# Another order of side work in an attention stage, a copy in two pieces and a power moved between two passes

## The chip, the cores and the metric

The kernel runs on one core of a Trainium2 chip. The metric is device time in microseconds (us) for one launch. A core has five engines with queues of their own: TensorE (PE) for matrix products, with its weight loads shown apart as PEld; VectorE (DVE); ScalarE (ACT); GpSimd (POOL); and SyncE (SP), which here only issues DMAs. Each engine works through its queue in order, and semaphores make it wait for the others.

## The reference

One inference step of a two-layer trunk for 128 context tokens and 512 latent tokens, width 1024, in float32. Layer 0 is gated grouped-query attention (16 heads, 4 key/value heads, head width 64), layer 1 a gated linear recurrence (HGRN2) in two directions. Cut to what matters here:

```python
for i in range(DEPTH):
    sh_p, sc_p, g_p = _adaln(c_ctx, ada_w[i], ada_b[i])        # shift, scale, gate
    hp = xp * (1.0 + sc_p) + sh_p                              # latent tokens alike
    if i % N_MIXERS == 0:
        out_p, kp, vp = _attn_context(hp, attn_w_in[j], ...)   # q, k normalised, rotary
        out_s = _attn_latent(hs, cache_k[:, j], cache_v[:, j], attn_w_in[j], ...)
    else:
        out_p, sp_fw, sp_bw = _rec_mix(hp, zeros, zeros, rec_w_in[j], ...)
        out_s, _, _ = _rec_mix(hs, state_rec[:, j, 0], state_rec[:, j, 1], ...)
    xp = _layer_norm(DEEPNORM_ALPHA * xp + g_p * out_p, ln_gain[i], ln_bias[i])
    xs = _layer_norm(DEEPNORM_ALPHA * xs + g_s * out_s, ln_gain[i], ln_bias[i])
```

Attention's inner step is `softmax(q @ k.T / sqrt(d)) @ v`; its result is multiplied by `silu(g)` and projected. The recurrence's result is RMS-normalised per head, multiplied by `silu(g)` and projected.

## The kernel before, in words

Tokens are tiled in five tiles of 128 (tile 4 holds the context tokens). Most products are made with both operands split into a high part of reduced precision and a low remainder, as three matmuls: high by high, high by low, low by high. So weights and activations are "split" before use: a copy to the high part on ACT (L242, L1133, L1562) and a subtraction for the low part on DVE or POOL (L243, L1134, L1563).

**Attention.** Work goes by units: one query head with 256 queries, or the context queries of four heads. A unit has two fronts and a back. A front makes a score tile `sc` on PE (L896, L897), its negative row maximum `nm` on DVE (L991), the exponentials `p` with their sums `su` on ACT (L996), the reciprocal `rc` on DVE (L1001) and the scaling of `p` on POOL (L1002). The back transposes `p` on PE into `pt` (L1009), copies it to `pts` on ACT or, for the last quarter, on DVE (L901), and for each pair of units multiplies with the values into `pot` (L923). The product with the gate, `gs` (L928), is put off by `D_OUTS` steps. `att_gen` runs fronts two units ahead of backs.

**Side work.** Between these steps `weave` takes steps from a list of other jobs: for each of three further groups of four heads the q projection (`q_gen`: `qmm` on PE, L363 to L365, then norm and rotary on DVE, a split `qs`, transposes `qps`, L707, and the copy to `X`); inside it, at the spots of `FILL_AT`, the modulation matmuls (`ada_gen`, `adaps`, L286) or, for the third group, ten column jobs (`cols_gen`, `spill`, L335, each a 128x1024 multiply with accumulation on DVE); then the first output weights (`wohi`, `wolo`) and the splits of `gs` into `hhi` and `hlo` (L1133, L1134). How many side steps follow each attention step is written as a string of digits, `SIDE_AT`. A compile-time scheduler then orders all of this first half on every engine, so the string shifts rows in all queues.

Score tiles share two PSUM buffers, `pt`, `qmm`, `qps` and `adaps` share three, `pot` has one.

**The tail.** The last head's recurrence ends with five transposes `oT` (L1561), the copy to `ghi` on ACT (L1562) and the remainder `glo` on DVE (L1563). The output projection `outp` (L1185 to L1187) has by then done all other heads for tiles 0 to 2. Class `Out` makes residual and layer norm: the product with the gate (L1231), the residual sum (L1234), sums on ACT (L1241, L1249), small statistics (L1245, L1246), a power on POOL for the reciprocal deviation (`rstdl`: L192 on DVE, then L193), and two passes over the two halves (L1268, L1270), with a DMA for each half (L1271).

Of the kernel before, what the change touches and what calls it, by code (L numbers as in the profile page):

```python
# [11 lines left out]
F32 = mybir.dt.float32  # L12
F32R = mybir.dt.float32r
U8 = mybir.dt.uint8
AF = mybir.ActivationFunctionType
ALU = mybir.AluOpType
AX = mybir.AxisListType

P = 128
# [4 lines left out]
NT = TT * P  # L24
# [4 lines left out]
RH = 8  # L29
# [4 lines left out]
ALPHA = 4.0 ** 0.25  # L34
HALVES = ((0, 320), (320, 640))
RAW_AHEAD = 2
FILL_AT = {1: '0a0b0e2e4e', 2: '0b0e2e4e', 3: '0b0e4e'}
LEAD = (1, 1)
RAW_START = 8
EARLY = 2  # L40
WARM = (8, 2, 3)
D_SCALE = 2
D_OUTS = 2
SIDE_T = 2.2
SIDE_AT = (
    "0101101011111000110110101101011011010110111001101021010010110110"
    "1001011010210101200101002011110100110101101002011000121110001101"
    "0110110101101002002110010110101101102002011101000001201101011")
D_GLA = 6.0
D_LEV = 2.3  # L50
D_KT = 2.0
# [78 lines left out]
def drain(gen):  # L130
    for _ in gen:
        pass
# [3 lines left out]
def hybrid_step(ctx: ExitStack, tc: tile.TileContext, a: dict, o: dict):  # L136
    nc = tc.nc
# [11 lines left out]
    def bank2(name):  # L149
        return pools["b2"].tile([P, 2, 512], F32, tag="b2", name=name)  # L150
# [38 lines left out]
    def rsqrt(out, in_, scale, eps, op=ALU.mult):  # L189
        n = in_.shape[-1]  # L190
        t = tiny.tile([P, NKV * TT], F32, tag="rs", name="rs_t")
        nc.vector.tensor_scalar(t[:, :n], in_, scale, eps, op, ALU.add)  # L192
        nc.gpsimd.tensor_tensor(out, t[:, :n], mhalf[:, :n], ALU.pow)  # L193
# [524 lines left out]
    def q_gen(c, X, fill):  # L718

        w = Weights("attn_w_in", c, (nc.vector, nc.vector), tuple(last_split))  # L720
        yield
        spots = {FILL_AT[c][i:i + 2] for i in range(0, len(FILL_AT[c]), 2)}
        pend = None
# [182 lines left out]
    def defer(n, fn):  # L906
        if n == 0:
            fn()
        else:
            later.append([n, fn])  # L910
# [14 lines left out]
    def av_out(pot, gt):  # L925
        tv = pot[:, :CW]
        tv = tv.rearrange("p (a b) -> p a b", a=2) if len(gt.shape) == 3 else tv
        defer(D_OUTS, lambda: tc.keep_in_program_order(nc.vector.tensor_tensor(gt, tv, gt, ALU.mult)))  # L928

# [206 lines left out]
    def split_gs(ks):  # L1136
        for k in ks:
            split_act(hhi[:, k, :], hlo[:, k, :], gs[:, k, :], nc.gpsimd if k < 6 else nc.vector)
            yield
# [49 lines left out]
    class Norm:  # L1189
# [15 lines left out]
        def finish(self):  # L1205
            y = self.y
            mv = tiny.tile([P, 2], F32, tag="mv", name="mv")
            nc.vector.bn_aggr(mv, self.st[:].rearrange("p a b -> p (a b)"))
            rt = tiny.tile([P, 8], F32, tag="rstd", name="rstdl")
            rstd = rt[:, 0:1]  # L1210
            rsqrt(rstd, mv[:, 1:2], 1.0, LN_EPS)
            for nh in range(2):
                s = slice(nh * 512, (nh + 1) * 512)
                nc.vector.tensor_scalar(y[:, s], y[:, s], mv[:, 0:1], rstd, ALU.subtract, ALU.mult)
            nc.sync.dma_start(x1d[self.tt], y)

    class Out:
# [43 lines left out]
                self.mean, self.op = self.st[:, 0, 1:2], ALU.add  # L1261
                rsqrt(self.rs, self.st[:, 1, 1:2], self.st[:, 1, 2:3], LN_EPS, ALU.add)

        def finish(self):
            x, y = self.x, self.y
            hs = [slice(nh * 512, (nh + 1) * 512) for nh in range(2)]
            for s in hs:
                nc.vector.scalar_tensor_tensor(x[:, s], y[:, s], self.mean, lng[:, s], self.op, ALU.mult)  # L1268
            for nh, s in enumerate(hs):
                nc.vector.scalar_tensor_tensor(x[:, s], x[:, s], self.rs, lnb[:, s], ALU.mult, ALU.add)  # L1270
                (nc.scalar if self.last and nh else nc.sync).dma_start(yd[self.tt][:, s], x[:, s])  # L1271

    drain(split_gs(range(6, 8)))
    drain(wo_gen(0, PIECES[4:], wob))
# [23 lines left out]
    def wide(ps):  # L1298
        return ps[:].rearrange("p a b -> p (a b)")
# [134 lines left out]
    ghi = hp.tile([P, KT, NT], F32R, tag="hhi", name="ghi")  # L1434
    glo = hp.tile([P, KT, NT], F32R, tag="hlo", name="glo")
# [4 lines left out]
    ngain = h1p.tile([P, 1], F32, name="ngain")  # L1440
# [5 lines left out]
    def gla_gen(h, H):  # L1446
# [25 lines left out]
        for lev in range(7):  # L1472
            nb = NT // (2 * w)
            pt = wide(bank2("lv"))
# [23 lines left out]
            if lev == 4:  # L1498
                pt = wide(bank2("dg"))
# [27 lines left out]
        for i in range(3):  # L1527
            nc.vector.scalar_tensor_tensor(S[:, 0, i + 1, :], S[:, 0, i, :], cur[:, i:i + 1], spv[:, i * P:(i + 1) * P],
                                           ALU.mult, ALU.add)
            c = 3 - i  # L1530
# [27 lines left out]
        pt = bank2("oT")  # L1558
        for c in range(TT):
            cc = slice(c * P, (c + 1) * P)  # L1560
            nc.tensor.transpose(wide(pt)[:, cc], on[:, cc], ident)  # L1561
        nc.scalar.activation(ghi[:, h, :], wide(pt)[:, :NT], AF.Copy, scale=ngain[:, 0:1])  # L1562
        nc.vector.scalar_tensor_tensor(glo[:, h, :], wide(pt)[:, :NT], ngain[:, 0:1], ghi[:, h, :].bitcast(F32),  # L1563
                                       ALU.mult, ALU.subtract)
        yield 0.0

    class Residual:
# [48 lines left out]
    for h in range(RH):  # L1616
        H = {} if h else H
        for dt in proj_gen(h, H, False) if h else first:
            lane.advance(dt)
        lane.add(gla_gen(h, H))  # L1620
# [70 lines left out]
    o3 = Out(3, outs[3])  # L1691
# [11 lines left out]
    o2 = Out(2, outs[2])  # L1703
# [2 lines left out]
    out_mms(o4.ps, 4, 0, ghi, glo)  # L1706
    for out in (o3, o2):
        out.spread()
    for out in (o3, o2):
        out.rstd()  # L1710
        out.finish()
    o4.half(both[0])
    for c in (slice(0, CW), slice(CW, 512)):
        if c.start:
# [88 lines left out]
```

## Time and profile before

| | us |
|---|---|
| median of the runs (3) | 839.59 |
| lowest and highest | 836.24, 839.99 |
| the profiled execution, own time | 837.36 |
| its span, first to last instruction | 835.6 |

The page gives, for each engine, its busy time and share of the span, and the busy share in 40 equal slices. A group's row gives line, engine, operation, names (out<-in), shapes and count, then busy time, mean ns of one, and the engine's idle time before it with the releaser. A row of the timeline gives start, duration and, in brackets, how long the engine stood idle just before and what ended that.

### The profile page before, as it was taken

To read this page: it belongs to the slowest core of one execution; us is meant where nothing else is said; L and a number is where in the kernel's file an instruction comes from. 1 tells how busy PE (TensorE), PEld (TensorE's weight loads), DVE (VectorE), ACT (ScalarE), POOL (GpSimd) and SP (SyncE) were. 2 spreads that over 40 slices of the span, in tenths; PEclk is the share of its full clock that TensorE was granted. 3 is DMA by queue.
4 is the path that set the end of the run, shared out by engine and by line. 5 is a ranking of instruction groups with operands and counts; after the bars stand their busy time and mean duration, and the time that the engine had idled before them with its cause. 6 is when DMAs were issued, how large, how long until landed. Compare 5 with 4: busy or idle time off the path is not lost.

```text
span 835.6 us, 19217 instructions
## 1 busy us (share of the span) xinstructions
PE 806.7 (97%) x8025; PEld 727.9 (87%) x8025; DVE 563.3 (67%) x996; ACT 386.6 (46%) x782; POOL 212.5 (25%) x261
## 2 busy tenths in 40 slices
PE   8999999999999889999999999999999999999994
PEld 6789999878889666889999999999999999998774
DVE  4567767675776995676356685758667575848477
ACT  2252545574667685232444444344444444445232
POOL 0123001452444752100001324042333223021121
PEclk9999999999999999999999999999999999999998
DMA  9943245223130242611313223232412313324041
GB/s 329 397 159 131 102 152 179 101 84 121 72 107 1 76 177 67 210 77 61 101 52 103 83 60 96 76 109 66 119 58 93 100 53 96 116 68 155 29 156 75
DMA packets 34326, 93.28 MB, mean 112 GB/s; under 512 B 5040, under 2 KB 12224, under 8 KB 34240
## 3 DMA queue, kind: packets, MB, share of 16 engines
q1 hardware_dynamic: 23568, 74.10, 25.5%
q0 software_dynamic: 4768, 14.18, 5.4%
q10 hardware_dynamic: 5904, 3.78, 1.5%
q8 instruction: 63, 1.03, 0.5%
q14 instruction: 23, 0.19, 0.1%
HBM read 82.85 MB, written 9.19 MB: 110 GB/s over the span
## 4 chain that ended last, share of the span: by engine, by line
PE 82%; DVE 9%; issue 3%; ACT 2%; DMA 1%; POOL 1%; SPq 0%; DVEq 0%; ACTq 0%; POOLq 0%
PE rps L1346 7%; PE rps L1347 7%; PE rps L1348 7%; PE vgps L1336 5%; PE vgps L1338 5%; PE vgps L1337 5%; PE outp L1185 4%; PE pot L923 4%; PE outp L1187 3%; PE outp L1186 3%; PE pt L1009 3%; PE lv L1479 2%; PE acc L541 2%; PE sc L896 2%; PE qmm L364 2%
## 5 line engine op out<-in xcount | busy, mean ns | idle before, releaser
L1346 PE MATMUL rps<-h1hi,rhi 128*128 128x320 f32 x368 | 118.3, 321 | 0.0
L1347 PE MATMUL rps<-h1lo,rhi 128*128 128x320 f32 x368 | 113.8, 309 | 0.0
L1348 PE MATMUL rps<-h1hi,rlo 128*128 128x320 f32 x368 | 113.6, 309 | 0.0
L1002 POOL TENSOR_SCALAR p<-p,rc 128x640 f32<-128x640 f32 x64 | 56.1, 880 | 128.8 <-DVE rc L1001 106.5
L1346 PEld LDWEIGHTS rps<-h1hi,rhi 128*128 128x128 f32 x368 | 69.1, 188 | 1.3
L1347 PEld LDWEIGHTS rps<-h1lo,rhi 128*128 128x128 f32 x368 | 69.2, 188 | 0.0
L1348 PEld LDWEIGHTS rps<-h1hi,rlo 128*128 128x128 f32 x368 | 69.1, 188 | 0.0
L243 DVE TENSOR_TENSOR rlo<-raw,rhi 128x1024 fp32r<-128x1024 f32 x32 | 45.0, 1408 | 34.0 <-ACT rhi L242 34.0
L991 DVE TENSOR_REDUCE nm<-sc 128x1 f32<-128x640 f32 x64 | 52.1, 816 | 19.8 <-PE sc L897 19.5
L1507 POOL COPY At<-near 32x160 f32<-32x160 f32 x32 | 13.5, 422 | 195.1 <-DVE near L1469 194.1
L996 ACT ACTIVATE p<-sc,nm 128x640 f32<-128x640 f32 x64 | 51.2, 800 | 21.9 <-DVE nm L991 15.2
L242 ACT CAST rhi<-raw 128x1024 fp32r<-128x1024 f32 x32 | 33.6, 1049 | 52.8 <-PE rps L1347 49.8
L1457 ACT COPY kc<-A 128x640 f32<-128x640 f32 x40 | 32.2, 806 | 54.6 <-DVE A L1488 50.8
L1336 PE MATMUL vgps<-rhi,h1hi 128*128 128x256 f32 x180 | 51.5, 286 | 0.0
L1009 PE MATMUL pt<-small,p 128*128 128x128 f32 x320 | 48.7, 276 | 2.7 <-POOL p L1002 1.8
L1337 PE MATMUL vgps<-rlo,h1hi 128*128 128x256 f32 x180 | 50.9, 283 | 0.0
L1338 PE MATMUL vgps<-rhi,h1lo 128*128 128x256 f32 x180 | 50.8, 282 | 0.0
L901 ACT COPY pts<-pt 128x512 f32<-128x512 f32 x64 | 35.9, 590 | 22.7 <-PE pt L1009 22.6
L896 PE MATMUL sc<-kk,X 128*128 128x320 f32 x128 | 43.1, 344 | 3.3 <-ACT p L996 3.0
L1009 PEld LDWEIGHTS pt<-small,p 128*128 128x128 f32 x320 | 37.0, 140 | 9.0 <-issue 3.4
L1336 PE MATMUL vgps<-wspare,h1hi 128*128 128x256 f32 x140 | 41.7, 298 | 0.0
L354 PE MATMUL gps<-hhi,whi 128*128 128x320 f32 x128 | 40.0, 312 | 0.1
(303 smaller groups left out, 2419.2 us busy)
## 6 DMA issues: line engine op xcount, KB each, us to landing
raw<-in_rec_w_in SPq DMA_DIRECT2D x40, 512.0 KB, 3.6
raw<-in_ada_m SPq DMA_DIRECT2D x16, 512.0 KB, 8.1
raw<-in_attn_w_in SPq DMA_DIRECT2D x16, 512.0 KB, 4.5
raw<-in_ada_s SPq DMA_DIRECT2D x16, 512.0 KB, 4.0
adaraw<-in_ada_c SPq DMA_DIRECT2D x11, 512.0 KB, 5.3
raw<-in_attn_w_out SPq DMA_DIRECT2D x8, 512.0 KB, 3.3
raw<-in_rec_w_out SPq DMA_DIRECT2D x8, 512.0 KB, 3.5
raw<-in_ada_c SPq DMA_DIRECT2D x5, 512.0 KB, 4.4
```

Of the source, the lines that this page charges most:

```text
L243: (lo_eng or nc.gpsimd).tensor_tensor(lo, raw, hi.bitcast(F32), ALU.subtract)
L896: nc.tensor.matmul(out, X[:, h, t0:t0 + P], kk[:, c, k0:k1], start=True, stop=False)
L991: nc.vector.tensor_reduce(nm[:, 0:1], sc[:, :, :320], AX.XY, ALU.max, negate=True)
L996: return nc.scalar.activation(halves(p[:]), sc[:, :, :320], AF.Exp, bias=nm[:, 0:1], accum_out=su[:, 0:1])
L1002: nc.gpsimd.tensor_scalar(p, p, rs[:, 0:1], 1.0, ALU.mult, ALU.mult)
L1009: nc.tensor.transpose(pt[:, i * 256 + q * P:i * 256 + (q + 1) * P], ps[q][:, (k0 + i) * P:(k0 + i + 1) * P], ident)
L1336: nc.tensor.matmul(out, h1hi[:, k, t], hi, start=(k == 0), stop=False)
L1337: nc.tensor.matmul(out, h1hi[:, k, t], lo, start=False, stop=False)
L1338: nc.tensor.matmul(out, h1lo[:, k, t], hi, start=False, stop=(k == KT - 1))
L1346: nc.tensor.matmul(ps[:, j, :320], hi[:, k, :], h1hi[:, k, t], start=(k == 0), stop=False)
L1347: nc.tensor.matmul(ps[:, j, :320], hi[:, k, :], h1lo[:, k, t], start=False, stop=False)
L1348: nc.tensor.matmul(ps[:, j, :320], lo[:, k, :], h1hi[:, k, t], start=False, stop=(k == KT - 1))
```

## The change

Three constants of the attention's schedule are replaced: the digits of `SIDE_AT` (both lists have 189 digits that sum to 117), the spots of `FILL_AT`, and `D_OUTS`. The last head's copy to `ghi` and its remainder are made in two pieces, the first for token tile 0. In the tail, the power of tile 2 is queued between the two last passes of tile 3.

```diff
-FILL_AT = {1: '0a0b0e2e4e', 2: '0b0e2e4e', 3: '0b0e4e'}
+FILL_AT = {1: '0b0e2e', 2: '0b0e2e4e', 3: '0a0b0e2e4e'}
...
-D_OUTS = 2
+D_OUTS = 1
...
-    "0101101011111000110110101101011011010110111001101021010010110110"
+    "0100021120010100020100012001210201010101000002111001021000000130"
...
-        def finish(self):
+        def finish(self, between=None):
...
+                if between and not nh:
+                    between()
...
-        nc.scalar.activation(ghi[:, h, :], wide(pt)[:, :NT], AF.Copy, scale=ngain[:, 0:1])
-        nc.vector.scalar_tensor_tensor(glo[:, h, :], wide(pt)[:, :NT], ngain[:, 0:1], ghi[:, h, :].bitcast(F32),
-                                       ALU.mult, ALU.subtract)
+        for c in ((slice(0, P), slice(P, NT)) if h == RH - 1 else (slice(0, NT),)):
+            nc.scalar.activation(ghi[:, h, c], wide(pt)[:, c], AF.Copy, scale=ngain[:, 0:1])
+            nc.vector.scalar_tensor_tensor(glo[:, h, c], wide(pt)[:, c], ngain[:, 0:1], ghi[:, h, c].bitcast(F32),
+                                           ALU.mult, ALU.subtract)
...
-    for out in (o3, o2):
-        out.rstd()
-        out.finish()
+    o3.rstd()
+    o3.finish(o2.rstd)
+    o2.finish()
```

On DVE, behind the last q projection's norm, the order was this (`spill` is a column job, `nm` the maximum of a score tile):

```order
L646 TENSOR_TENSOR qn<-r,rstd 128x256
L991 TENSOR_REDUCE nm<-sc 128x1
L335 SCALAR_TENSOR_TENSOR spill,shsc_80<-raw,silb 128x1024
L1001 RECIPROCAL rc<-su 128x1
L699 TENSOR_TENSOR qs_3527<-qn,qs_3527 128x4x64
L901 COPY pts<-pt 128x256
L991 TENSOR_REDUCE nm<-sc 128x1
L335 SCALAR_TENSOR_TENSOR spill,shsc_80<-raw,silb 128x1024
L1001 RECIPROCAL rc<-su 128x1
L335 SCALAR_TENSOR_TENSOR spill,shsc_80<-raw,silb 128x1024
L991 TENSOR_REDUCE nm<-sc 128x1
L335 SCALAR_TENSOR_TENSOR spill,shsc_80<-raw,silb 128x1024
```

Now, at the same place of the same engine:

```order
L646 TENSOR_TENSOR qn<-r,rstd 128x256
L991 TENSOR_REDUCE nm<-sc 128x1
L1001 RECIPROCAL rc<-su 128x1
L335 SCALAR_TENSOR_TENSOR spill,shsc_80<-raw,silb 128x1024
L901 COPY pts<-pt 128x256
L991 TENSOR_REDUCE nm<-sc 128x1
L699 TENSOR_TENSOR qs_3543<-qn,qs_3543 128x4x64
L335 SCALAR_TENSOR_TENSOR spill,shsc_80<-raw,silb 128x1024
L1001 RECIPROCAL rc<-su 128x1 x2
L335 SCALAR_TENSOR_TENSOR spill,shsc_80<-raw,silb 128x1024
L991 TENSOR_REDUCE nm<-sc 128x1
L335 SCALAR_TENSOR_TENSOR spill,shsc_80<-raw,silb 128x1024 x2
```

Before, seven spills stood behind this projection's first rotary row (L630); now five do, and four of those follow within eight rows.

On PE, behind the last head's transposes, tiles 0, 1 and 2 were served in turn (`w` are the last output weights):

```order
L1561 MATMUL oT<-small,on 128x128 x5
L1185 MATMUL outp<-w_9466,ghi 128x512
L1186 MATMUL outp<-w_9467,ghi 128x512
L1185 MATMUL outp<-w_9466,ghi 128x512
L1186 MATMUL outp<-w_9467,ghi 128x512
L1185 MATMUL outp<-w_9466,ghi 128x512
L1187 MATMUL outp<-w_9466,glo 128x512
L1185 MATMUL outp<-w_9467,ghi 128x512
L1186 MATMUL outp<-w_9467,ghi 128x512
L1187 MATMUL outp<-w_9467,glo 128x512
```

Now PE has this there:

```order
L1563 MATMUL oT<-small,on 128x128 x5
L1185 MATMUL outp<-w_9466,ghi 128x512
L1186 MATMUL outp<-w_9467,ghi 128x512
L1187 MATMUL outp<-w_9466,glo 128x512
L1185 MATMUL outp<-w_9467,ghi 128x512
L1186 MATMUL outp<-w_9467,ghi 128x512
L1187 MATMUL outp<-w_9467,glo 128x512
```

Tile 0's six matmuls now come first; before, its sixth was the ninth row.

On DVE in the tail, the powers' first step (L192) of tiles 3 and 2 stood so:

```order
L192 TENSOR_SCALAR rs_t<-st 128x1
L1231 TENSOR_TENSOR y<-outp,gate_9381 128x512
L1270 SCALAR_TENSOR_TENSOR x_9835<-x_9835,rstdl,ln_9841 128x512 x2
L192 TENSOR_SCALAR rs_t<-st 128x1
L1234 SCALAR_TENSOR_TENSOR y<-x_9839,y 128x512
L1270 SCALAR_TENSOR_TENSOR x_9837<-x_9837,rstdl,ln_9841 128x512 x2
```

Now they stand so:

```order
L192 TENSOR_SCALAR rs_t<-st 128x1
L1231 TENSOR_TENSOR y<-outp,gate_9381 128x512
L1270 SCALAR_TENSOR_TENSOR x_9837<-x_9837,rstdl,ln_9843 128x512
L192 TENSOR_SCALAR rs_t<-st 128x1
L1270 SCALAR_TENSOR_TENSOR x_9837<-x_9837,rstdl,ln_9843 128x512
L1270 SCALAR_TENSOR_TENSOR x_9839<-x_9839,rstdl,ln_9843 128x512 x2
L1234 SCALAR_TENSOR_TENSOR y<-x_9841,y 128x512
```

The second power moved ahead of one pass, and the residual sum L1234 of the last tile moved behind both passes that need that power.

More of the change, by code (lines that the diff above doesn't have):

```diff
@@ L42 @@
 D_SCALE = 2
-D_OUTS = 2
+D_OUTS = 1
 SIDE_T = 2.2
 SIDE_AT = (
-    "0101101011111000110110101101011011010110111001101021010010110110"
-    "1001011010210101200101002011110100110101101002011000121110001101"
-    "0110110101101002002110010110101101102002011101000001201101011")
+    "0100021120010100020100012001210201010101000002111001021000000130"
+    "2002020010001200011201020101300010100102000000201112120001100001"
+    "3100002000111000000310010102010113001000012000120300210000012")
 D_GLA = 6.0
```

## The prediction

> **What bounds the kernel now.** I read the page's engine shares first, then the slices, then the stretches around the changed places, then the waits inside them.
>
> ```profile
> PE 806.7 (97%) x8025; PEld 727.9 (87%) x8025; DVE 563.3 (67%) x996; ACT 386.6 (46%) x782; POOL 212.5 (25%) x261
> PE   8999999999999889999999999999999999999994
> DVE  4567767675776995676356685758667575848477
> ```
>
> PE is busy for 97% of the span, so an edit pays only where PE stands still. The slices show two such places: slices 14 and 15, where DVE reads 9, and the last one. Both are touched by the change. The stretches put numbers on it; the columns are length, then busy time of PE, PEld, DVE, ACT, POOL.
>
> ```profile
> 134.20:270.80 136.60, 134.43 (x1131) 114.13 (x1130) 93.12 (x203) 83.90 (x189) 56.41 (x62) 1.00 0.25 86
> 270.80:303.40 32.60, 27.22 (x206) 21.16 (x205) 30.92 (x60) 24.72 (x52) 22.93 (x21) 1.00 0.35 126
> 303.40:328.60 25.20, 22.85 (x173) 16.21 (x172) 15.88 (x35) 16.68 (x41) 9.00 (x11) 1.00 0.12 48
> 328.60:795.80 467.20, 465.22 (x5353) 436.03 (x5354) 306.30 (x485) 197.56 (x379) 100.87 (x142) 1.00 0.29 93
> 795.80:835.60 39.80, 27.23 (x143) 23.18 (x143) 29.94 (x61) 11.69 (x33) 5.93 (x8) 0.91 0.29 107
> ```
>
> Attention runs from 134.2 to 328.6. The last q projection (qmm) ends at 270.8; until then PE idles 2.2 us (136.60 - 134.43), afterwards 5.4 + 2.35 = 7.7 us, and DVE fills 30.92 of 32.60 us. The long middle stretch holds no edited row. In the last 39.8 us PE is not the bound: DVE is.
>
> Who ends PE's waits in attention (engine, line, releaser: total, times, longest):
>
> ```profile
> PE sc L896 <- ACT p L996: 3.0, 5, 1.0
> PE qps L707 <- DVE qs L699: 2.4, 1, 2.4
> PE pt L1009 <- POOL p L1002: 1.8, 3, 0.9
> PE pot L923 <- DVE pts L901: 0.8, 2, 0.5
> PE pt L1009 <- ACT pts L901: 0.7, 2, 0.5
> PE outp L1185 <- DVE gs L928: 0.5, 1, 0.5
> ```
>
> They sum to 9.2 us, and that is about the most that a new order of attention can win.
>
> **The side list, FILL_AT and D_OUTS.** No computation is added; 117 side steps are spread over the same 189 attention steps. What moves is best seen from the ten column jobs on DVE (spill, L335). Prices in the late stretch, as groups (busy, mean ns), and the spills' shortest, median and longest:
>
> ```profile
> L991 DVE TENSOR_REDUCE nm<-sc 128x1 f32<-128x640 f32 x16 | 12.9, 810 | 3.3 <-PE sc L897 3.3
> L335 DVE SCALAR_TENSOR_TENSOR spill<-raw,silb 128x1024 f32<-128x1024 f32 x7 | 10.0, 1429 | 0.0
> L243 DVE TENSOR_TENSOR wolo<-raw,wohi 128x1024 fp32r<-128x1024 f32 x4 | 5.9, 1472 | 0.0
> L335 DVE SCALAR_TENSOR_TENSOR spill<-raw,silb x8: 1197/1208/2604, 265.1 to 293.3; 128x1024 f32<-128x1024 f32 x8
> ```
>
> Before, seven of the ten spills stand on DVE behind the last projection's first rope row (L630), now five. Two spills, 2 x 1.43 = 2.9 us, thus leave the stretch where DVE is full and enter one where it is 68% busy (93.12 of 136.60) and PE has projections to run. The four wolo splits stay where they were.
>
> How much of it PE gets back is bounded on both sides. At most the whole 2.9 us; at least nothing, because the remaining five spills are packed closer (four among eight rows, with only two of the maxima nm between them), so the score groups behind them wait as before. To choose, I laid out the changed rows by hand with row durations. PE's prices:
>
> ```profile
> 93.30 0.65 PE qps L707 x8
> 210.90 2.31 PE pot L923 x20
> 247.02 0.87 PE pt L1009 x8
> 308.53 0.31 PE L897 MATMUL sc<-klo,X 128*128 128x320 f32 x1
> 308.68 0.31 PE L896 MATMUL sc<-kk,X 128*128 128x320 f32 x1
> ```
>
> The two score rows start 0.15 us apart, a transpose costs 0.87/8 = 0.11, a pot group 2.31. From the last projection's end to the first output matmul PE has 84 sc, 124 pt and ptp, seven pot groups, 12 qps and 12 short rows: 12.4 + 13.5 + 16.2 + 1.0 + 1.8 = 44.9 us of work in 57.8 us (270.8 to 328.6), so 12.9 us go to waits and handovers. Now there are 80 sc and 128 pt: 44.7. In my layout, pot_3647 waits 1.1 us for a copy (pts) that stands behind a spill, the next unit's last transposes 1.1 us for a copy behind two spills, and two score groups about 0.9 us each for exponentials behind two weight casts on ACT. At the point that PE reached at 303.4, it comes out 1.0 us earlier. I take **-1.5 us**, between this and the whole 2.9.
>
> Before the last projection the new list mostly lengthens leads: counting PE rows at these prices between a score group and the first transpose that needs it, the middle group has 12.5 us instead of 7.9. That bears on the waits for POOL's p and ACT's p, which are 4.8 us over the whole of attention. PE idles only 2.2 us there; I take **-0.7** (bounds -2.2, all of that idle time, and +1.0, one more wait as long as the longest of these). D_OUTS puts each product (L928) one step earlier in DVE's queue, at no cost: same rows, and the pot bank frees sooner. SP's load order is unchanged. On POOL the four gated stores move among the scalings:
>
> ```profile
> 171.94 2.12 POOL L327 DMA_DIRECT2D gated<-acc x4
> ```
>
> The scalings behind them wait up to 2.1 us, less than the longer lead covers; without that lead it would be PE's.
>
> **The split copy.** The last head's chain:
>
> ```profile
> 795.81 0.74 PE L1561 MATMUL oT<-small,on 128*128 128x128 f32 x5
> 796.58 0.79 ACT L1562 ACTIVATE ghi<-oT,ngain 128x640 fp32r<-128x640 f32 x1 [3.34 <-PE oT L1561]
> 797.43 0.50 PE L1185 MATMUL outp<-w,ghi 128*128 128x512 f32 x1 [0.88 <-ACT ghi L1562]
> 799.82 0.69 DVE L1231 TENSOR_TENSOR y<-outp,gate 128x512 f32<-128x512 f32 x1 [1.52 <-PE outp L1187]
> 805.74 0.39 PE L1187 MATMUL outp<-w,glo 128*128 128x512 f32 x1
> 806.44 0.68 DVE L1231 TENSOR_TENSOR y<-outp,gate 128x512 f32<-128x512 f32 x1
> L1550 ACT ACTIVATE kt<-op 128x128 f32<-128x128 f32 x15 | 3.9, 281 | 11.9 <-PE op L1542 11.9
> ```
>
> A 128x128 piece costs ACT 0.28 instead of 0.79 us, so PE restarts 0.5 us earlier if the first piece waits for all five transposes, 0.9 if for one. PE then finishes token tile 0 with six matmuls instead of nine (by about 798.1 to 798.5), so DVE's first product comes 1.3 to 1.6 us earlier. But DVE has slack of only 0.31 us at its next need of PE: tile 3's first half ends at 806.13 (805.74 + 0.39) and is read at 806.44. So DVE gains 0.8 to 1.1 us there and keeps it, since its later rows are dense. The second piece costs ACT more in total, hidden beside those six matmuls (1.4 us); without them it would be PE's.
>
> **The moved power.**
>
> ```profile
> 820.50 1.41 DVE L1270 SCALAR_TENSOR_TENSOR x<-x,rstdl,ln 128x512 f32<-128x512 f32 x2
> 821.83 0.20 DVE L192 TENSOR_SCALAR rs_t<-st 128x1 f32<-128x1 f32 x1
> 821.96 0.68 DVE L1234 SCALAR_TENSOR_TENSOR y<-x,y 128x512 f32<-128x512 f32 x1
> 822.18 0.86 POOL L193 TENSOR_TENSOR rstdl<-rs_t,mhalf 128x1 f32<-128x1 f32 x1 [1.72 <-DVE rs_t L192]
> 823.08 1.41 DVE L1270 SCALAR_TENSOR_TENSOR x<-x,rstdl,ln 128x512 f32<-128x512 f32 x2 [0.44 <-POOL rstdl L193]
> ```
>
> The power now starts one pass (0.67 us) earlier, but the cover changes: before, L1234 (0.68) ran under it; now the second L1270 pass (0.67) does, and L1234 comes after. From L192 to the next L1270 it is 1.25 us either way, so DVE still waits about 0.45 us: **gain nothing**. Behind it, some rows now follow directly on the row that feeds them; I allow +0.1. The tail sums to **-0.9 us** (-1.1 to 0).
>
> **Sum.** -1.5 - 0.7 - 0.9 = -3.1 us. The profiled execution took 837.36 us (span 835.6 and 1.8 around it), which gives 834.3; the median of the runs shown is 839.59, 2.2 us higher, which gives 836.5. I forecast the middle, **835.4 us**, from a base of 838.5.
>
> **Rivals.**
> 1. *The longer leads clear most of attention's waits.* For it: each of the 9.2 us is a wait on something that a longer lead covers. Against it: the last unit has no projection left under it, and the final waits for pts and gs have the same rows. It gives 6 to 8 us with the tail, so 830.5 to 832.5.
> 2. *The side list does nothing.* The packed spills give back what the two early ones win; only the tail counts: 837.6.
> 3. *Slower: DVE and POOL block each other.*
>
> ```profile
> 280.32 1.55 POOL L1134 TENSOR_TENSOR hlo<-gs,hhi 128x640 fp32r<-128x640 f32 x1
> 280.35 2.60 DVE L335 SCALAR_TENSOR_TENSOR spill<-raw,silb 128x1024 f32<-128x1024 f32 x1
> 283.50 0.52 PE L707 MATMUL qps<-identr,qs 128*128 128x128 f32 x4 [2.44 <-DVE qs L699]
> ```
>
> This spill began 0.03 us after POOL's hlo and took 2.60 us; POOL ended at 281.87, and 1.1 us later the spill did. PE lost 2.44 us at qps behind it. [...] POOL's hlo rows now stand four in a row, the fifth near the packed spills. If all five late spills meet POOL rows and wait 1.4 us each, that is 7.0 us where the seven lost 1.6 (7 x (1.43 - 1.20)); +5.4 on a full DVE, with the tail +4.5: 843. It decides from about three blocked spills on. [...]
>
> **How the numbers follow.** Forecast 0.46 (834 to 837.5; a tenth of all cases lies past the bound), rival 1 0.28, rival 2 0.12, rival 3 0.14 (nearly all past it). What a measurement can tell from no change is 0.5%, 4.2 us: faster 0.10 + 0.28 = 0.38, slower 0.12, same 0.50. The range 830.0 to 841.0 takes in rival 1, rival 2 and the milder half of rival 3; the forecast's own is 834 to 837.5.
>
> **What would show it.** PE's idle time between the last projection and the first output matmul falls from 7.7 to about 6 us; below 3 is rival 1, above 9 rival 3. Late spills show 1.2 us each, or 2.6 for rival 3. PE's wait for ghi falls from 0.88 to under 0.4 us, and DVE's read of tile 3 comes about 0.9 us sooner after oT. The wait for the second rstdl stays at 0.4 to 0.5; if it goes, my cover was wrong. The forecast fails if attention's PE waits change by over 4 us either way.

## The result, and the profile after

| | before | after |
|---|---|---|
| median of the runs (4 each), us | 839.52 | 831.83 |
| lowest and highest | 836.24, 839.99 | 831.35, 833.04 |
| the profiled execution, own time | 837.36 | 831.35 |
| its span | 835.6 | 829.6 |

After over before is 0.9929, with a 95% interval of 0.9907 to 0.9951: faster by about 0.7%. The forecast was 835.4, so the direction was right and the change was larger than forecast.

The two profiled executions are laid side by side in stretches, cut at the start of the first and last gate matmul (`gps`), the last projection matmul (`qmm`), the first output matmul (`outp`) and the last head's transposes (`oT`), and behind DVE's last row:

| stretch | before, us | after, us | change |
|---|---|---|---|
| start to first gate matmul | 71.49 | 70.50 | -0.99 |
| gate matmuls | 62.69 | 63.06 | +0.37 |
| last gate matmul to last projection | 136.54 | 134.77 | -1.77 |
| last projection to first output matmul | 57.89 | 55.47 | -2.42 |
| middle, no edited row | 467.19 | 466.55 | -0.64 |
| `oT` to DVE's last row | 34.46 | 33.91 | -0.55 |
| rest | 5.33 | 5.33 | 0 |

They sum to -6.0 us. Attention carries -4.19, the tail -0.55. The first row isn't the change's: all engines have the same order up to the first gate matmul, and over the twelve kernels profiled here that share this order it took between 70.28 and 73.31 us. The middle varied between 466.37 and 467.85 in the same way. The tail repeats much better: it took 33.88 to 33.91 in all five profiles that have both of its edits, and 34.45 to 34.48 in all that have neither.

The page of the changed kernel, engine shares and slices:

```profile
PE 803.0 (97%) x8025; PEld 725.2 (87%) x8025; DVE 559.9 (67%) x997; ACT 386.8 (47%) x783; POOL 214.0 (26%) x261
...
PE   8999999999999899999999999999999999999994
...
DVE  4567767675777975775456685657667685858486
```

DVE still reads 9 in slice 14, but 7 instead of 9 in slice 15, though it has one row more in all. The stretches of attention, first of the kernel before (cut again at the exact points), then after; the columns are length, then busy time of PE, PEld, DVE, ACT and POOL, the granted PE clock, and the DMAs' share and rate:

```profile
134.19:270.73 136.54, 134.37 (x1131) 114.07 (x1130) 93.13 (x203) 83.83 (x189) 56.34 (x61) 1.00 0.25 86
270.73:328.62 57.89, 50.14 (x380) 37.45 (x378) 46.80 (x94) 41.49 (x92) 31.99 (x33) 1.00 0.25 92
```

```profile
133.56:268.32 134.76, 133.28 (x1130) 113.63 (x1129) 94.74 (x210) 84.19 (x191) 55.89 (x62) 1.00 0.27 91
268.32:323.79 55.47, 49.37 (x379) 37.20 (x378) 41.79 (x87) 41.18 (x90) 33.32 (x32) 1.00 0.27 86
```

Length less PE's busy time is PE's idle time. It fell from 2.17 to 1.48 us in the first stretch and from 7.75 to 6.10 in the second, together 2.34. The other 1.85 us are in a place that the prediction didn't look at: PE's *busy* time fell by 1.09 and 0.77, although over the whole of attention PE runs the same 1505 rows in both kernels, kind for kind.

PE's waits in attention, by line and releaser (total, times, longest), after:

```profile
PE pot L923 <- DVE pts L901: 2.0, 2, 1.5
PE sc L896 <- ACT p L996: 1.6, 4, 0.7
PE pt L1009 <- DVE pts L901: 1.2, 2, 1.0
PE pt L1009 <- ACT pts L901: 0.9, 2, 0.5
PE pt L1009 <- POOL p L1002: 0.7, 1, 0.7
PE outp L1185 <- DVE gs L928: 0.5, 1, 0.5
PE pscp L896 <- ACT p L996: 0.3, 1, 0.3
```

They sum to 7.2 us instead of 9.2. The single wait of 2.4 us for `qs` is gone, and waits for `pts` have grown. The longest wait is now 1.5 us. The column jobs, as a group (shortest, median and longest in ns), and then the first of the late ones with POOL's rows beside it:

```profile
L335 DVE SCALAR_TENSOR_TENSOR spill<-raw,silb x10: 1209/1224/1726, 233.2 to 286.1; 128x1024 f32<-128x1024 f32 x10
```

From the timeline, start and duration:

```profile
278.25 1.51 DVE L335 SCALAR_TENSOR_TENSOR spill<-raw,silb 128x1024 f32<-128x1024 f32 x1
...
278.66 2.50 POOL L1134 TENSOR_TENSOR hlo<-gs,hhi 128x640 fp32r<-128x640 f32 x1
...
281.14 5.58 POOL L1002 TENSOR_SCALAR p<-p,rc 128x640 f32<-128x640 f32 x3
```

No spill takes 2.6 us any more (the longest 1.73). But DVE and POOL still collide. At the first late spill DVE's row came first, and it is POOL's that is held up (2.50 instead of 1.55). The next three scalings of `p` on POOL then take 5.58 us together (2.02, 1.76 and 1.84), where the median of all 64 is 0.80, and two of the spills beside them take 1.60 and 1.73. Before, two scalings that ran beside spills took 1.62 each.

The tail, start, duration and, in brackets, the idle time before:

```profile
790.34 0.74 PE L1563 MATMUL oT<-small,on 128*128 128x128 f32 x5
...
791.12 0.37 ACT L1565 ACTIVATE ghi<-oT,ngain 128x128 fp32r<-128x128 f32 x1 [3.34 <-PE oT L1563]
...
791.53 0.50 PE L1185 MATMUL outp<-w,ghi 128*128 128x512 f32 x1 [0.46 <-ACT ghi L1565]
...
791.90 0.69 ACT L1565 ACTIVATE ghi<-oT,ngain 128x512 fp32r<-128x512 f32 x1 [0.42 <-DVE glo L1566]
...
792.62 0.75 DVE L1566 SCALAR_TENSOR_TENSOR glo<-oT,ngain,ghi 128x512 fp32r<-128x512 f32 x1 [0.76 <-ACT ghi L1565]
...
800.29 0.69 DVE L1231 TENSOR_TENSOR y<-outp,gate 128x512 f32<-128x512 f32 x1 [0.29 <-PE outp L1187]
...
815.02 0.21 DVE L192 TENSOR_SCALAR rs_t<-st 128x1 f32<-128x1 f32 x1
...
816.33 1.42 DVE L1270 SCALAR_TENSOR_TENSOR x<-x,rstdl,ln 128x512 f32<-128x512 f32 x2 [0.44 <-POOL rstdl L193]
```

PE's wait for `ghi` went from 0.88 to 0.46, and PE restarts 1.19 us after `oT` instead of 1.62. DVE's read of tile 3 stands at `oT` + 9.95 instead of + 10.63. DVE's first product of tile 0 isn't among these rows; it moved from `oT` + 4.01 to + 2.95. The wait for the second `rstdl` is 0.44 in both.

### The profile page after: what moved, and what is told of

It reads as the page before. It is cut to its first block, busy times and chain, and to the rows that moved or that the text cites. A ratio compares the mean times of both kernels' runs of the same rounds, so it can differ in the third digit from the quotient of the medians.

```text
span 829.6 us, 19207 instructions
## 1 busy us (share of the span) xinstructions
PE 803.0 (97%) x8025; PEld 725.2 (87%) x8025; DVE 559.9 (67%) x997; ACT 386.8 (47%) x783; POOL 214.0 (26%) x261
## 4 chain that ended last, share of the span: by engine, by line
PE 86%; DVE 7%; DMA 2%; issue 2%; POOL 1%; ACT 1%; SPq 0%; DVEq 0%; ACTq 0%; POOLq 0%
PE rps L1348 7%; PE rps L1349 7%; PE rps L1350 7%; PE vgps L1338 5%; PE vgps L1340 5%; PE vgps L1339 5%; PE pot L923 4%; PE outp L1185 4%; PE outp L1187 4%; PE outp L1186 4%; PE pt L1009 4%; PE lv L1481 2%; PE acc L541 2%; PE sc L896 2%; PE sc L897 2%; PE qmm L363 2%
## 5 line engine op out<-in xcount | busy, mean ns | idle before, releaser
L243 DVE TENSOR_TENSOR rlo<-raw,rhi 128x1024 fp32r<-128x1024 f32 x32 | 45.0, 1409 | 33.8 <-ACT rhi L242 33.8
L923 PE MATMUL pot<-pts,vv 128*64 128x256 f32 x320 | 38.3, 384 | 2.1 <-DVE pts L901 2.0
```

The lines of the kernel that those rows point to most:

```text
L923: nc.tensor.matmul(pot[j * HD:(j + 1) * HD, :CW], vv[:, slot, c * HD:(c + 1) * HD], moving[j], start=first, stop=last)
```

## The experiments

Attention's length, from the last gate matmul to the first output matmul, is read from each run's profile. It repeats well: 194.43 us before, and 194.46 in the first experiment, whose attention is unedited. The last column is worked out from windows of 2.5 us: the sum of (1 - granted clock) x 2.5 over attention. Each row is one profiled execution; three executions with all three constants lost 0, 1.7 and 1.7 us of clock, as is shown at the end.

| kernel | to last projection | from there | sum | clock lost |
|---|---|---|---|---|
| before | 136.54 | 57.89 | 194.43 | 0 |
| after | 134.77 | 55.47 | 190.24 | 0 |
| all three constants, old tail | 134.81 | 56.02 | 190.83 | 1.7 |
| fill spots alone | 139.05 | 60.90 | 199.95 | 3.4 |
| side digits alone | 135.09 | 60.97 | 196.06 | 1.7 |
| D_OUTS alone | 137.53 | 60.04 | 197.57 | 3.4 |
| digits and spots | 134.73 | 58.51 | 193.24 | 0 |

### Tail alone, and constants alone

The tail alone is the changed kernel with this:

```diff
-FILL_AT = {1: '0b0e2e', 2: '0b0e2e4e', 3: '0a0b0e2e4e'}
+FILL_AT = {1: '0a0b0e2e4e', 2: '0b0e2e4e', 3: '0b0e4e'}
-D_OUTS = 1
+D_OUTS = 2
...
-    "0100021120010100020100012001210201010101000002111001021000000130"
+    "0101101011111000110110101101011011010110111001101021010010110110"
...
```

> Only the tail's two edits (copy in two pieces, moved power); the attention's three constants as before. Theory A (the parts add up, the tail is worth what the profile of the changed kernel shows from oT to DVE's last row): 0.4 to 0.9 us faster, DVE's last row at oT + 33.9 instead of + 34.5. Rival B (the tail has nothing to do with it, what looked like its gain is variation): within 0.2 us, last row at oT + 34.4 or later. Rival C (the tail carries a third or more of the change): over 2 us faster.

Measured: median 838.33 us (12 runs) against 838.44, ratio 0.9997 (0.9982 to 1.0011). In the profile DVE's last row came at `oT` + 33.88 instead of 34.46, so 0.58 us were gained there. The profile bears out theory A, of a size that the times can't tell from nothing. Theory C is excluded.

The constants alone are the kernel before with the three constants of the change and nothing else.

> Only the three constants of attention (side list, fill spots, D_OUTS); the tail as before. Theory A: attention carries the rest of the change, 4.2 us in the profile between the last gate matmul and the first output matmul, and up to 6 if the stretches without edited rows (1.3 us shorter in the profile) belong to it: 834 to 835.5 us against 839.5. Rival B (the 1.3 us at the start and in the middle are variation between executions): 4.2 us and no more, and those two stretches come out as before. Rival C (tail carries it): under 2.5 us.

Measured: 833.85 us (6 runs), ratio 0.9949 (0.9929 to 0.997); attention 190.83, 3.6 shorter. The start took 70.32 and the middle 467.47, so the middle's 0.6 of the changed kernel didn't come back: it was variation. Attention carries the change.

### The fill spots alone, the digits alone

```diff
-FILL_AT = {1: '0a0b0e2e4e', 2: '0b0e2e4e', 3: '0b0e4e'}
+FILL_AT = {1: '0b0e2e', 2: '0b0e2e4e', 3: '0a0b0e2e4e'}
```

> Only the fill spots of before replaced: two of the seven late column jobs (spill) now stand ahead of the last projection's rope rows; the digits of the side list as before. Theory A, as forecast (spills out of the stretch where DVE is full): 1.0 to 2.9 us faster, nearly all of it between the last projection and the first output matmul. Rival D (one collision: the spill of 2.60 us beside POOL's hlo and the qps wait of 2.44 us behind it are what went, and any shift does that): 2 to 2.7 us, qps wait gone, and side digits alone do the same. Rival E (longer leads do it): within 0.7 us.

Measured: 844.62 us (6 runs), ratio 1.0081 (1.0061 to 1.0102): **slower**, though two of the seven late spills had left, as in the changed kernel. All three theories missed, and PE's wait for `qs`, 2.2 us, was still there. On ACT of this kernel, and then on PE:

```profile
299.74 1.04 ACT L242 CAST wohi<-raw 128x1024 fp32r<-128x1024 f32 x1 [4.14 <-DMA raw<-in_attn_w_out]
300.69 0.58 ACT L901 COPY pts<-pt 128x512 f32<-128x512 f32 x1
...
301.41 0.45 PE L1009 MATMUL pt<-small,p 128*128 128x128 f32 x1 [4.04 <-ACT pts L901]
```

ACT stood 4.14 us at a weight cast whose load had not landed. The copy that PE needed was the next row in its queue. Then the clock fell; windows of PE, with its granted clock third from the end:

```profile
297.50:300.00 2.50, 0.00 (x0) 0.00 (x0) 1.58 (x3) 0.27 (x1) 0.45 (x1) 0.92 1.01 403
300.00:302.50 2.50, 0.84 (x2) 0.58 (x3) 1.63 (x3) 2.50 (x6) 0.00 (x0) 0.50 0.40 162
302.50:305.00 2.50, 2.50 (x11) 2.42 (x11) 0.90 (x2) 1.91 (x5) 1.79 (x2) 0.50 0.63 210
305.00:307.50 2.50, 2.50 (x16) 2.20 (x16) 1.66 (x4) 2.19 (x6) 2.11 (x3) 0.72 0.00 0
```

The four windows sum to 3.4 us of clock lost (2.5 x (0.08 + 0.50 + 0.50 + 0.28)) behind a wait of 4.0. If the clock was either whole or one half, which is an estimate from these windows, it was at one half from about 299.6 to 306.4.

The digits alone are the kernel before with the new `SIDE_AT`.

> Only the digits of the side list replaced; fill spots and D_OUTS as before, so seven spills still stand behind the last projection's rope. Theory A, as forecast: 0.7 us faster (between 2.2 faster and 1.0 slower), nearly all of it ahead of the last projection's end. Rival D (one collision): 2 to 2.7 us faster, with no spill over 2 us and no qps wait of 2.4 us. Rival E (longer leads): 2.5 us or more, spread over attention's waits for p.

Measured: 841.52 us (12 runs), ratio 1.0043 (1.0028 to 1.0057): slower too. To the last projection attention was 1.45 shorter (136.54 to 135.09), within what theory A gave for the leads; behind it, 3.1 longer. PE's long wait for `qs` and the spill of over 2 us were gone, as rival D asked, and no time was won. Neither a single collision (D) nor longer leads (E) makes the gain by itself. The profiled execution was the fastest of the twelve (839.08), so its +1.6 us is low for this kernel: the ratio of the times is worth 3.6.

### Digits and spots together, D_OUTS alone

> Side digits and fill spots replaced together, D_OUTS and tail as before. Read by the length from the last gate matmul to the first output matmul (194.4 us before, 190.8 with all three constants, 200.0 with the fill spots alone, 196.1 with the digits alone). Theory F (digits and spots are one setting: they only fit each other, D_OUTS adds little): 190 to 192. Rival G (the three are additive, so D_OUTS must be worth some -10): 201 to 202. Rival H (half and half): 195 to 198.

Measured: attention 193.24 (a single run, 837.1 us), between the bounds of F and H. Together the two gain 1.2 where one alone loses 5.5 and the other 1.6.

> Only D_OUTS from 2 to 1, the rest as before. The same length, 194.4 us before. Theory F, and the prediction (no cost, no gain of its own): 193.5 to 195. Rival G: 184 to 186. Rival H: 190 to 193.

Measured: attention 197.57, so 3.1 *longer* (a single run); no theory had it. On top of digits and spots the same constant takes 193.24 down to 190.24 to 190.83 (the three kernels that have all three). Of the 3.1, 1.0 came ahead of the last projection with no clock lost, and 2.1 behind it, where 3.4 us of clock were lost. So the constant isn't free, and its effect depends on the list; how much of the 2.1 another execution would repeat is open. The window behind the 2.4 us wait for `qs` of this kernel:

```profile
282.50:285.00 2.50, 1.53 (x10) 1.56 (x11) 2.50 (x7) 0.65 (x2) 0.90 (x1) 0.76 0.40 129
285.00:287.50 2.50, 2.50 (x14) 1.88 (x15) 2.50 (x7) 1.90 (x4) 1.62 (x1) 0.56 0.23 87
```

and the kernel before, at the same place behind the same wait:

```profile
282.50:285.00 2.50, 1.50 (x13) 1.52 (x14) 2.50 (x7) 0.94 (x2) 0.89 (x1) 1.00 0.40 143
285.00:287.50 2.50, 2.50 (x25) 1.62 (x23) 2.50 (x7) 1.39 (x4) 1.62 (x1) 1.00 0.21 74
```

The same wait was followed by a loss of 1.7 us of clock (2.5 x (0.24 + 0.44)) in one execution and of none in the other, nor in the first experiment's, which has it too: 24 rows pass in 5 us, or 38.

### The power where it was

```diff
-    o3.rstd()
-    o3.finish(o2.rstd)
-    o2.finish()
+    for out in (o3, o2):
+        out.rstd()
+        out.finish()
```

> The changed kernel with the tail's power where it stood before (the split copy stays). Length from the last head's transposes to DVE's last row, 34.46 us before, 33.9 with both edits. Prediction (the moved power gains nothing, and the dependent rows behind it cost 0.1): 33.8, with DVE's wait for the second rstdl still 0.4 to 0.5. Rival (the power carries the gain of the tail): 34.4. Rival (the split is worth the 0.9 forecast and the moved power takes 0.35 of it back): 33.55.

Measured: 33.77 us from `oT` to DVE's last row, with the wait for the second `rstdl` at 0.44. So the split copy alone gains 0.69 (34.46 - 33.77), and the moved power gives back 0.14 (33.91 - 33.77), well over the 0.03 by which the tail of one kernel varied. The prediction held in kind and nearly in size.

### The fill spots without the wait for the load

In the kernel with the fill spots alone:

```diff
...
-        raw = raw[:, :hi.shape[-1]]
+        raw = last_raw[0] = last_raw[0] if src == ("attn_w_out",) + PIECES[3] else raw[:, :hi.shape[-1]]
```

> The kernel with the fill spots alone, whose fourth piece of output weights is cast from the third piece's buffer instead of its own (so that piece's values are not the reference's); its load is still issued, but ACT's cast no longer waits for it. Theory J (the loss of the fill spots is ACT's queue standing still 4.1 us for that load, with the copies that PE needs behind it): the length from the last gate matmul to the first output matmul falls from 200.0 by 3 to 5, to 195 to 197, and PE's wait of 4.0 us for pts goes. Rival K (the loss is spread over many waits): 199 or more.

Measured: attention 199.50 instead of 199.95. The wait of 4.0 us for `pts` went, and theory J fell nevertheless: PE's waits for POOL's `p` grew from nothing to 2.3 us, and the clock lost 3.4 us again. With the load out of the way, the scheduler put the last two weight splits (`wolo`, L243) one behind the other on DVE:

```profile
295.63 3.61 POOL L1002 TENSOR_SCALAR p<-p,rc 128x640 f32<-128x640 f32 x2 [4.14 <-PE sc L897]
...
296.29 2.36 DVE L243 TENSOR_TENSOR wolo<-raw,wohi 128x1024 fp32r<-128x1024 f32 x2 [0.69 <-ACT wohi L242]
...
299.29 0.33 PE L1009 MATMUL pt<-small,p 128*128 128x128 f32 x1 [1.83 <-POOL p L1002]
```

The first of POOL's two scalings took 0.8 us. The second, begun 0.1 us behind DVE's pair, took 2.8, ended 0.6 us after it, and PE waited 1.83 us for it. DVE's order differs in 18 places from the kernel with the fill spots alone, so this run doesn't hold the order fixed; it shows that the load wasn't the only thing due there.

### The spills cut to a sixteenth

In the kernel before and in the changed one:

```diff
-        for c in range(2):
+        for c, n in ((0, D if after else 64), (1, D if after else 64)):
...
-                nc.vector.scalar_tensor_tensor(spill(), raw, 1.0, silb[:, c, :], ALU.mult, ALU.mult,
+                nc.vector.scalar_tensor_tensor(spill()[:, :n], raw[:, :n], 1.0, silb[:, c, :n], ALU.mult, ALU.mult,
```

> The kernel before with its ten late column jobs (spill) cut from 1024 to 64 columns, so the layer-1 modulation is not the reference's; the scheduler redraws the order a little. Length from the last gate matmul to the first output matmul, 194.4 us before. Theory L (what separates the two kernels is where the spills stand on a full DVE): it falls by 4 to 7, to 187.5 to 190.5. Rival M (it is the order of all the other rows): by 0 to 3, to 191.5 or more.

> The same cut in the changed kernel (190.2 us there). Theory L: the gap to the kernel before closes, both cut kernels within 1.5 us of each other. Rival M: the cut kernels stay 3 to 5 us apart.

Measured: 196.37 (136.26 + 60.11) and 194.04 (135.99 + 58.05), so 1.9 and 3.8 us *longer* than with the whole spills (a single run each), although DVE has 7 and 2.6 us less to do behind the last projection:

```profile
269.76:329.88 60.12, 53.21 (x380) 38.43 (x378) 39.54 (x94) 41.17 (x92) 29.26 (x32) 0.97 0.26 88
```

```profile
270.87:328.92 58.05, 49.87 (x375) 36.73 (x373) 39.23 (x89) 41.36 (x92) 29.22 (x31) 1.00 0.25 82
```

The two are 2.3 apart, between L and M, but L's main claim, that attention gets shorter by the time taken out of the spills, is gone. In the first of them the weight casts now come sooner than their loads:

```profile
286.81 1.04 ACT L242 CAST wohi<-raw 128x1024 fp32r<-128x1024 f32 x1 [1.65 <-DMA raw<-in_attn_w_out]
...
288.49 1.06 PE L1009 MATMUL pt<-small,p 128*128 128x128 f32 x8 [2.04 <-ACT pts L901]
```

The scheduler redraws some rows for the shorter spills, so these two runs don't hold the order fixed.

### One column job fewer in attention

```diff
-COLS_LATE = 5
+COLS_LATE = 4
```

> The changed kernel with COLS_LATE 4 instead of 5: one more column job (two spills) is done beside the gate matmuls, ahead of attention, and two fewer stand in it. Theory L: the length from the last gate matmul to the first output matmul falls by 1 to 2.9, to 187.3 to 189.2, and the gate stretch (63.1 us) grows by less than 0.5, since DVE is 70% busy there: 829 to 831 us against 831.8. Rival M (placement of all rows, digits set for ten late spills): 190 to 194, no gain or slower.

Measured: 833.96 us (10 runs), ratio to before 0.9951 (0.9937 to 0.9965). Behind the last projection 54.00 instead of 55.47, as theory L says for two spills fewer; ahead of it 136.11 instead of 134.77, because the extra job came last beside the gate matmuls, waited 0.39 us for its own load, and held up the first projection's split:

```profile
PE qmm L364 <- DVE wlo L243: 1.7, 1, 1.7
```

Together 190.11, no gain over the changed kernel and within rival M's range. The next kernel has `COLS_LATE = 4` too, and starts the column jobs beside the gate matmuls earlier:

```diff
-ROWS_AT = (0, 0, 0, 0, 1, 1, 2, 2, 2, 2, 2, 2, 2, 2, 2, 0)
+ROWS_AT = (0, 0, 2, 2, 2, 2, 2, 2, 2, 2, 2, 2, 2, 0, 0, 0)
```

> The kernel with COLS_LATE 4, and the column jobs beside the gate matmuls started two gate steps earlier (ROWS_AT), so that no spill stands between the last gate matmul and the split (wlo) for which the first q projection waited 1.7 us in the run with COLS_LATE 4 alone. Theory P (that wait was the whole price of the extra job there): the length from the last gate matmul to the last projection goes from 136.1 back to 134.8, the one from there to the first output matmul stays at 54.0, together 188.8 against 190.2 in the changed kernel; the time 1 to 2 us below the changed kernel's. Rival Q (the order is redrawn and gives it back elsewhere): 190 or more in sum, or a gate stretch over 63.6.

Measured: attention 134.81 + 53.95 = 188.76, just what theory P says, the shortest of all. But the gate stretch grew to 65.45, which is Q's second case: 833.6 us (8 runs), ratio to before 0.9952 (0.9936 to 0.9968). The windows at the place where PE waited 1.9 us for `qs`, with column jobs moved up on DVE ahead of it:

```profile
85.00:87.50 2.50, 0.84 (x6) 0.58 (x4) 1.44 (x4) 0.94 (x2) 0.00 (x0) 1.00 0.00 0
87.50:90.00 2.50, 2.21 (x12) 2.03 (x13) 2.43 (x5) 1.17 (x2) 0.00 (x0) 0.61 0.00 0
90.00:92.50 2.50, 2.50 (x14) 2.50 (x13) 0.89 (x2) 1.13 (x2) 0.00 (x0) 0.70 0.01 3
```

Here 1.7 us of clock went with the wait. No kernel of these was shown to be faster than the changed one.

## Why the prediction was right in direction and short in size

**What bounds the kernel.** Right: PE stays at 97%, the time came from attention and the tail, and the middle varied without a change of its rows. The forecast's own range, 834 to 837.5, doesn't hold the measured 831.83; only the part of the range that was there for rival 1 does, and that is luck, as is told below.

**The term of attention, -2.2, measured -4.19: the step that failed.** Three things in it:

- *Size.* The term was read from PE's idle time alone ("that is about the most that a new order of attention can win", of the 9.2 us of waits; "all of that idle time" as the bound before the last projection). The idle time did what the forecast said: -0.69 for -0.7, and -1.65 for -1.5 (7.75 to 6.10, "from 7.7 to about 6"). And the sign of failure that was named, PE's waits changing by over 4 us, didn't come: they fell by 2.0 while attention fell by 4.2, so that sign couldn't see what was missed. The missing 1.85 us are PE's busy time for the same rows. PE's rows overlap: `sc` rows start 0.15 us apart and last 0.31, so when the next `sc` row has to wait, the one before it counts as busy for 0.16 us past the usual start (0.31 - 0.15), and a stop shorter than that doesn't show as idle. This can be counted by starts. Take as usual the spacing that three in four rows of a line and shape keep: the starts that came over 0.2 us later than that were 19 with 13.1 us of delay before, and 16 with 10.3 after, 2.8 of the 4.2. So starts show more than idle time does; that short stops are all of the rest is argued, not shown.
- *Reason.* "Two spills ... leave the stretch where DVE is full" was taken as the cause of the -1.5. Doing that by the fill spots alone lost 5.5 us, and cutting the spills to a sixteenth lost 1.9 and 3.8. It held where two more spills were taken out of the changed kernel: -1.5 behind the last projection, twice. That -1.65 of idle time met the -1.5 is thus in part luck, for the reason given doesn't bring it about by itself. Nor is a full engine by itself the bound: DVE had 11 to 21 us to spare over that stretch in every kernel (57.89 - 46.80 before, 60.12 - 39.54 with the short spills).
- *D_OUTS* "at no cost: same rows, and the pot bank frees sooner" was wrong. With it alone attention took 3.1 more, 1.0 of it where no clock was lost; on top of digits and spots it took 2.4 to 3.0 less.

In the place of the sum of moved rows, the runs show that digits, spots and D_OUTS are one setting: alone +5.5, +1.6 and +3.1, two together -1.2, all three -3.6 to -4.2. The first three have 1.7 to 3.4 us of lost clock in them; even with all of it taken off, they come to about +1.8 together, not -4.2. What each row's place contributes isn't settled. Three things by which a list out of step can lose are seen in the traces: a queue in order that stands at a row whose data come late, with a needed row behind it (ACT 4.14 us at the weight cast, DVE 0.39 us at the extra column job); DVE and POOL holding each other up (a spill of 2.60 us where the median is 1.21, an `hlo` of 2.50 where it is 1.56); and the clock behind a wait (1.7 or 3.4 us lost). What each is worth isn't settled either: with the wait for the weight cast taken away, attention won only 0.45 us, since POOL's row came late in its stead.

**The tail, -0.9, measured -0.55.** The mechanism was right, two sizes were off. The first piece costs 0.37 us, not the 0.28 of L1550, and PE restarts 0.43 sooner, not 0.5 to 0.9, since the piece waits for all five transposes (it starts 0.78 us behind `oT`, the whole copy did at 0.77). So tile 3's first half is ready 0.41 sooner, DVE's slack of 0.31 turned into a wait of 0.29, and DVE reads it 0.68 sooner, not 0.8 to 1.1. DVE's first product comes 1.06 sooner, not 1.3 to 1.6: the second `glo` stands ahead of it. The second piece stayed hidden, as forecast, though it waits 0.42 for DVE's first `glo`, which the forecast hadn't seen. The moved power gained nothing and the dependent rows behind it cost 0.14 (forecast 0.1).

**The rivals.** Rival 1's time (830.5 to 832.5) is the one that came, but not by its mechanism: 7.2 of the 9.2 us of waits are still there, and PE's idle time is 6.1, not below 3. Rival 2 is excluded by the constants alone. Rival 3's collisions did come, but smaller: of the five late spills one took 1.51 us, one 1.60 and one 1.73, so 0.3 to 0.5 more, not 1.4, and the others 1.21 and 1.23. Not every pair of rows collides: in the kernel before, the five maxima that ran beside POOL's rows between 271.6 and 280.4 kept their 0.80 to 0.83 us. But the forecast priced only POOL's `hlo`, and its scalings of `p` collide with spills too (two took 1.62 us each beside spills in the kernel before; the median of all 64 is 0.80).

**The base.** The forecast took the middle between the profile's 837.36 and the median. In the later sets of runs, on three chips, the same kernel had medians of 838.44, 838.29 and 837.5, so part of the difference of the first medians (7.7) is this spread; the profiles' 6.0 less the 1.3 us of start, gate and middle is 4.7, and the constants alone timed 0.51% (4.3 us).

## What to carry to other kernels

An order made by a scheduler from a table of numbers is one setting here: price the whole of it from its own queues, not as a sum of rows moved; each part by itself made attention longer. Work taken off a full engine paid in two kernels here (1.5 us behind the last projection) and lost in three others, where a weight cast on ACT waited for its load (4.14, 1.65 and 0.8 us); look for the row behind which a queue will stand next. And read what a reorder may win on PE from the spacing of its starts too, because its idle time showed only 2.3 of 4.2 us here.

## What the runs showed of the hardware

**Behind some of PE's waits the granted clock fell to one half.** In these profiles the granted clock of attention's windows is 1.00, except behind some waits: there the windows sum to a loss of 1.7 us, in the kernel with D_OUTS alone and in the one without the wait for the load twice that in two falls, and behind the wait of 4.0 us 3.4 us in one. Windows that lie wholly in such a fall show 0.50. The clock fell behind single waits of 2.4 us (with D_OUTS alone, and not in the kernel before and in the one with the tail alone) and of 1.9 us (to 0.61 and 0.70 in two windows of the gate stretch, in the kernel with the earlier column jobs). It also fell where no wait was as long: in the run with the power where it was, behind 0.75 and 0.98 us of PE's idle time in two windows of 2.5 us, and in the one with the constants alone behind 1.22 and 0.59. The windows of the first of these two:

```profile
290.00:292.50 2.50, 1.75 (x13) 1.07 (x11) 2.50 (x6) 2.21 (x3) 1.45 (x3) 1.00 0.33 93
292.50:295.00 2.50, 1.52 (x8) 1.48 (x8) 2.50 (x7) 2.50 (x6) 0.56 (x1) 0.75 0.75 264
295.00:297.50 2.50, 2.24 (x10) 1.44 (x9) 2.50 (x7) 1.57 (x4) 0.98 (x2) 0.56 0.89 283
```

The changed kernel has waits of 0.55, 0.21 and 0.98 us within 3.0 us there (287.5 to 290.6), and lost no clock. The three kernels with the changed attention lost 0, 1.7 and 1.7 us of clock and took 190.24, 190.83 and 190.34, so the two that lost clock took 0.6 and 0.1 us longer. What decides whether the clock falls behind a wait was not shown.

**Spills on DVE and `hlo` on POOL held each other up, either way round.** Before, the spill that began 0.03 us behind POOL's `hlo` took 2.60 us (the median there is 1.21); after, POOL's `hlo` that began 0.41 us behind the spill took 2.50 (median 1.56). The cut spills show it most plainly. In the changed kernel with spills of 64 columns, one took 0.20 us, and the next, which began 0.01 us behind POOL's row of 1.55, took 1.62 and ended 0.08 us behind it:

```profile
280.75 0.20 DVE L335 SCALAR_TENSOR_TENSOR spill<-raw,silb 128x64 f32<-128x64 f32 x1
...
281.69 1.55 POOL L1134 TENSOR_TENSOR hlo<-gs,hhi 128x640 fp32r<-128x640 f32 x1
...
281.70 1.62 DVE L335 SCALAR_TENSOR_TENSOR spill<-raw,silb 128x64 f32<-128x64 f32 x1
```
